# Three edits at once: first loads in pieces, the order of block products and roots at the second norm, and the final norm of a column chunk placed under the next chunk's products

## The chip, the cores and the metric

The kernel runs on one core of a Trainium2 chip. The metric is device time in microseconds (us), from one launch to its end. The core has five engines that run in parallel, each through its own queue of instructions and in that queue's order: TensorE (PE, with its weight loads, PEld), VectorE (DVE), ScalarE (ACT), GpSimd (POOL) and SyncE (SP), which here only issues the transfers. An instruction that waits for a semaphore holds up everything behind it on its engine. TensorE is granted one of two clock levels, 1.2 or 2.4 GHz; the profile gives the granted clock as a share of the full one.

## The reference, cut to what matters

One layer of a decoder step, for a prompt of 1024 tokens and eight samples of eight tokens each, 1088 token columns in all, with a model width of 1024:

```python
h = rms_norm(x, norm_mix_g)                       # first norm
proj = h @ w_in                                   # conv values and gates, q, k, v
...                                               # causal conv head group, dilated attention
x = x + concat([a, o]) @ w_out
h = rms_norm(x, norm_ffn_g)                       # second norm
g = depthwise_conv(concat([past, h @ w_ffn_gate]))
x = x + (silu(g) * (h @ w_ffn_up)) @ w_ffn_down
y = rms_norm(x, norm_final_g)                     # final norm
```

`rms_norm(x, g)` is x times the reciprocal root of the mean square over the 1024 features of a token, times g.

## The kernel before

The activations are held with the features on the 128 partitions and the tokens along the columns, so that x is eight tiles of 128 x 1088. Every product is made of three matmuls with split operands: a "hi" part (`xh`, `wh`, rounded by ACT) and a "lo" part (`xl`, `wl`, the rest, by DVE or POOL), as hi x hi, lo x hi and hi x lo. A block of 1088 columns is cut into column chunks `CHUNKS` of 384, 384 and 320.

**The norms.** The sum of squares over the features is made of squares (ACT, some on POOL) that are added up elementwise over the eight tiles (`sqa`, `sq`; DVE, some on POOL). `root` then sums over the partitions with small matmuls against a column of ones (line 192, out into a bank `ss`, `g2` or `r`), and computes the reciprocal root with some short operations of DVE and one of ACT (lines 194 to 207). `spread` turns the root (`rr`) back into a 128-partition tile `rb` by transposes on PE (line 219) and a copy by ACT (line 221).

**The start.** Lines 263 to 273: SP issues x tile 0, the first block of `w_in` (512 KB in one transfer, by `load_w`), x tile 1, the second block, and the other x tiles, in this order by hand (`tc.issue_after` holds the scheduler to it); three loads of a cache (`cr`, 768 KB each) stand between tiles 4 and 5. Each x tile is split as a whole in `scaled_split`, and each weight block as a whole in `load_w`. `first_gemms` then runs over the eight tiles k, two weight blocks and three chunks: 144 matmuls, 18 for each k. The squares of x tiles 1, 3 and 5 are made on POOL.

**The second norm.** `out_half(h, hook)` makes the output projection of half the columns (544) as eight products m of 12 matmuls (`block_product`, lines 849 to 852, in matmuls of 272 columns), adds each to x (line 982), squares it (line 985) and adds it to the sum of the half (line 989). For the second half, a hook starts work on the norm of the first half: `root` after product m = 1, `spread` after product m = 4 (`norm_first`). What comes next are the first block products of the FFN (`b11h`, `px`, `py`, line 865), which need x scaled by `rb` (line 995). `two_products` fills two such outputs, tile by tile, as the tiles come.

**The end.** The last part of the down projection runs over four column chunks `TAIL` of 256, 256, 320 and 256; for each, `last_product` makes eight products m of 12 matmuls (lines 1262 to 1264), which DVE adds to x (line 1266), ACT squares (line 1268), and DVE and POOL add up in two sums (line 1273) that are joined at the end (line 1274). `last_norm` of a chunk is written in the program behind the next chunk's products; there the scheduler has put it where its operands come. It scales four tiles on DVE (line 1282) and four on POOL and ACT (lines 1284, 1285) and stores each (line 1286). Five banks `g` hold products, two banks `r` the roots.

Of the kernel before, what the change touches and what calls it, by code (L numbers as in the profile page):

```python
# [44 lines left out]
TAIL = ((0, 256), (256, 256), (512, 320), (832, 256))  # L45
# [12 lines left out]
WR = 2  # L58
# [19 lines left out]
def trunk_kernel(tc, xT, w_in, w_out, w_gate, w_up, w_down, par, kc, vc, sa, sf, pmask, smask,  # L78
                 yT, kT, vT, ca, cas, cf):
    nc = tc.nc  # L80
    with (
# [51 lines left out]
        nc.vector.memset(onesc, 1.0 / DC)  # L133

# [49 lines left out]

        def root(sq, div, width):
# [5 lines left out]
            for i, n in enumerate(size):  # L191
                nc.tensor.matmul(ps[:n, i:i + 1], sq[:, i * P:i * P + n], ones, start=True, stop=True)
# [14 lines left out]
            nc.vector.scalar_tensor_tensor(r, t, 1.5, r, op0=ALU.add, op1=ALU.mult)  # L207
            return r

        def spread(r, new, width):  # L210
# [3 lines left out]
            for c0 in range(0, width, 512):  # L214
                pb = bank(*rbank[0])
                w = min(512, width - c0)
                for i in range(c0 // P, -(-(c0 + w) // P)):
                    n = size[i]
                    nc.tensor.transpose(pb[:, i * P - c0:i * P - c0 + n], r[:n, i:i + 1].to_broadcast([n, P]),
                                        ident[:n, :n])  # L220
# [18 lines left out]
        def scaled_split(x, c):  # L239

            hi = zt(main[0], "X", 16, "xh", N, F32R)
            nc.scalar.activation(hi, x, AF.Copy, scale=c)
            lo = zt(main[0], "X", 16, "xl", N, F32R)
            nc.vector.scalar_tensor_tensor(lo, x, c, hi.bitcast(F32), op0=ALU.mult, op1=ALU.subtract)
            return hi, lo
# [17 lines left out]
        x0, w0 = [], []  # L263
        with ExitStack() as order:
            for k in range(KT):
                t = keep("x")
                opened = nc.sync.dma_start(t, xT[k * P:(k + 1) * P, :]).ins
                order.enter_context(tc.issue_after(opened))
                x0.append(t)
                if k in W0:  # L270
                    w0.append(load_w(w_in[2 - 2 * len(w0)], KT, nc.gpsimd if w0 else nc.vector))
        h = [scaled_split(x0[k], col(C_GMIX + k)) for k in range(KT)]
        R = rstd(sum_squares(x0, nc.vector, zbig, (1, 3, 5)), D, zbig)
# [581 lines left out]
        def two_products(outs, ws, x, start, hook=lambda k, last: None):  # L855
# [3 lines left out]
            nk = len(x)  # L859
            for k, (xh, xl) in enumerate(x):  # L860
                for o, (whi, wlo) in zip(outs, ws):
                    for c in range(2):
                        ps = o[:, PO:512] if c == 0 else o[:, 512:PO + HN]
                        t = slice(c * n, c * n + n)
                        nc.tensor.matmul(ps, whi[:, k, :], xh[:, t], start=(start and k == 0), stop=False,
                                         skip_group_check=True)
                        nc.tensor.matmul(ps, whi[:, k, :], xl[:, t], start=False, stop=False, skip_group_check=True)
                        last = nc.tensor.matmul(ps, wlo[:, k, :], xh[:, t], start=False, stop=(k == nk - 1),
                                                skip_group_check=True).ins
                hook(k, last)  # L870
# [385 lines left out]
        def last_product(t0, n):  # L1256
            acc = [None, None]
            for m in range(KT):
                ps = bank(*gbank[0])
                whi, wlo = w[m]  # L1260
                for k, (xh, xl) in enumerate(act):
                    nc.tensor.matmul(ps[:, :n], whi[:, k, :], xh[:, t0:t0 + n], start=(k == 0), stop=False)
                    nc.tensor.matmul(ps[:, :n], whi[:, k, :], xl[:, t0:t0 + n], start=False, stop=False)
                    nc.tensor.matmul(ps[:, :n], wlo[:, k, :], xh[:, t0:t0 + n], start=False, stop=(k == nj - 1))
                x = x2[m][:, t0:t0 + n]
                nc.vector.tensor_add(x, ps[:, :n], x)
                s = wide("sq")[:, :n]
                nc.scalar.activation(s, x, AF.Square)
                i = m % 2
                if acc[i] is None:  # L1270
# [117 lines left out]
```

## Time and profile before

| | before |
|---|---|
| median of 3 runs | 1409.12 us (1405.84 to 1413.22) |
| the profiled execution's own time | 1410.36 us |
| its span, first to last instruction | 1408.6 us |
| busy PE, DVE, ACT, POOL | 96%, 60%, 37%, 32% |
| mean granted TensorE clock | 0.982 |

The span is what the instructions take; 1.76 us of the execution's time lie outside it. PE is busy nearly all of the span, so what matters are the few places where it isn't, and the places at which its clock is at the lower level.

### The profile page before, as it was taken

The page shows a single profiled execution, that of the slowest core. Times are in us where ns is not written, and L with a number is a line of the kernel's source. Part 1 is how long each engine was busy: PE and PEld are TensorE (multiplying, and loading weights), DVE is VectorE, ACT ScalarE, POOL GpSimd, SP SyncE. Part 2 cuts the span into 40 slices and gives each one's busy share as a digit, 9 for nine tenths or more (in the row PEclk, how much of TensorE's full clock was granted, in tenths as well). Part 3 has the DMA queues.
Part 4 walks back from the last instruction along what each step waited for, and adds up shares of the span by engine and source line. Part 5 has one row for each costly group of instructions (what it writes and reads, how often), then busy time and mean ns, then how long its engine had stood idle before and what let it go on. Part 6 is the DMA issues. An engine that isn't in the chain of part 4 may idle for free.

```text
span 1408.6 us, 25028 instructions
## 1 busy us (share of the span) xinstructions
PE 1348.9 (96%) x10059; PEld 1282.0 (91%) x10059; DVE 844.7 (60%) x1636; ACT 521.9 (37%) x1047; POOL 447.0 (32%) x362
## 2 busy tenths in 40 slices
PE   6999999999998999988999999999999999999995
PEld 6988879899977777988999999999999999999995
DVE  7398595556674656677965555665655543322146
ACT  5312212456564564254533333333332332112033
POOL 3221111111001103330754654554654222233124
PEclk9999999999999999998999999999999999999998
DMA  7247676836798878450112222212222672313003
GB/s 275 57 140 248 222 256 206 224 111 168 197 266 229 256 213 257 128 195 24 47 50 89 93 77 77 92 47 77 92 78 77 202 275 60 117 57 123 12 16 113
DMA packets 84884, 195.17 MB, mean 139 GB/s; under 512 B 12576, under 2 KB 46752, under 8 KB 84768
## 3 DMA queue, kind: packets, MB, share of 16 engines
q1 hardware_dynamic: 84768, 193.57, 43.7%
q8 instruction: 79, 1.29, 0.4%
q14 instruction: 37, 0.30, 0.1%
HBM read 145.03 MB, written 48.52 MB: 137 GB/s over the span
## 4 chain that ended last, share of the span: by engine, by line
PE 76%; DVE 10%; issue 5%; DMA 5%; POOL 2%; ACT 1%; SPq 1%; POOLq 0%; DVEq 0%; ACTq 0%
PE g L174 10%; PE g L172 10%; PE g L173 10%; PE py L849 4%; PE py L851 4%; PE py L852 4%; DVE cacc L342 4%; PE o L675 3%; PE s L590 3%; PE pz L852 3%; PE pz L849 3%; PE pz L851 3%; PE px L849 3%; PE px L852 3%; PE px L851 3%
## 5 line engine op out<-in xcount | busy, mean ns | idle before, releaser
L148 POOL TENSOR_TENSOR wl<-wr,wh 128x768 fp32r<-128x768 f32 (+2 forms) x61 | 116.8, 1916 | 461.6 <-PE g L174 373.6
L172 PE MATMUL g<-xh,wh 128*128 128x384 f32 (+1 forms) x472 | 158.1, 335 | 0.0
L173 PE MATMUL g<-xl,wh 128*128 128x384 f32 (+1 forms) x472 | 156.6, 332 | 0.0
L174 PE MATMUL g<-xh,wl 128*128 128x384 f32 (+1 forms) x472 | 156.5, 332 | 0.0
L173 PE MATMUL g<-al,wh 128*128 128x384 f32 (+1 forms) x432 | 143.2, 332 | 1.7 <-DVE al L1203 1.7
L172 PE MATMUL g<-ah,wh 128*128 128x384 f32 (+1 forms) x432 | 141.6, 333 | 2.2 <-ACT ah L1202 0.8
L174 PE MATMUL g<-ah,wl 128*128 128x384 f32 (+1 forms) x432 | 142.7, 332 | 0.7 <-POOL wl L148 0.7
L146 ACT ACTIVATE wh<-wr 128x768 fp32r<-128x768 f32 (+2 forms) x62 | 52.0, 839 | 240.1 <-PE g L174 177.8
L939 POOL TENSOR_TENSOR wb<-wr,wb 128x512 fp32r<-128x512 f32 x84 | 115.2, 1383 | 56.8 <-ACT wb L938 56.8
L1225 DVE TENSOR_TENSOR x<-g,x 128x384 f32<-128x384 f32 (+1 forms) x72 | 38.0, 534 | 137.8 <-PE g L174 137.6
L938 ACT ACTIVATE wb<-wr 128x512 fp32r<-128x512 f32 x84 | 52.4, 628 | 164.2 <-DVE wr L954 105.0
L631 ACT ACTIVATE y<-y,m 128x128 f32<-128x128 f32 (+1 forms) x192 | 88.4, 463 | 32.2 <-DVE m L619 32.1
L1143 DVE SCALAR_TENSOR_TENSOR fc<-gb,prm,fc 128x1104 f32<-128x1104 f32 x44 | 83.5, 1918 | 14.7 <-ACT fc L1141 14.4
L174 PEld LDWEIGHTS g<-xh,wl 128*128 128x128 f32 x472 | 89.3, 189 | 2.6 <-issue 2.5
L172 PEld LDWEIGHTS g<-xh,wh 128*128 128x128 f32 x472 | 89.6, 190 | 1.4 <-issue 1.2
L173 PEld LDWEIGHTS g<-xl,wh 128*128 128x128 f32 x472 | 89.6, 190 | 1.1 <-issue 1.0
L594 DVE CUSTOM_DVE_ANT_0 y<-s,pmk 128x128 f32<-128x128 f32 (+1 forms) x192 | 63.9, 378 | 41.6 <-PE s L590 33.2
L939 POOL TENSOR_TENSOR wa<-wr,wa 128x512 fp32r<-128x512 f32 x42 | 54.9, 1308 | 101.0 <-ACT wa L938 101.0
L172 PEld LDWEIGHTS g<-ah,wh 128*128 128x128 f32 x432 | 81.7, 190 | 3.1 <-ACT ah L1202 1.1
L173 PEld LDWEIGHTS g<-al,wh 128*128 128x128 f32 x432 | 82.1, 190 | 2.4 <-DVE al L1203 2.4
L174 PEld LDWEIGHTS g<-ah,wl 128*128 128x128 f32 x432 | 82.1, 190 | 1.0 <-POOL wl L148 1.0
L342 DVE SCALAR_TENSOR_TENSOR cacc<-gp,prm,cacc 128x1024 f32<-128x1024 f32 x60 | 77.9, 1299 | 0.1
(358 smaller groups left out, 4133.0 us busy)
## 6 DMA issues: line engine op xcount, KB each, us to landing
cr<-in_kc SPq DMA_DIRECT2D x24, 768.0 KB, 8.4
cr<-in_vc SPq DMA_DIRECT2D x24, 768.0 KB, 7.1
kk<-dk SPq DMA_DIRECT2D x48, 256.0 KB, 7.5
u<-u SPq DMA_DIRECT2D x22, 544.0 KB, 3.2
ur<-u SPq DMA_DIRECT2D x22, 544.0 KB, 5.4
wr<-in_w_in SPq DMA_DIRECT2D x22, 512.0 KB, 5.2
wr<-in_w_gate SPq DMA_DIRECT2D x22, 512.0 KB, 3.3
wr<-in_w_up SPq DMA_DIRECT2D x22, 512.0 KB, 5.0
```

The lines of the kernel that those rows point to most:

```text
L148: lo_eng.tensor_sub(lo, raw, hi.bitcast(F32))
L172: nc.tensor.matmul(ps[c], whi[:, k, :], xh[:, t0:t0 + n], start=(k == 0), stop=False)
L173: nc.tensor.matmul(ps[c], whi[:, k, :], xl[:, t0:t0 + n], start=False, stop=False)
L174: nc.tensor.matmul(ps[c], wlo[:, k, :], xh[:, t0:t0 + n], start=False, stop=(k == nk - 1))
L342: eng.scalar_tensor_tensor(acc[:, :S], gp[:, j:j + S], col(w0 + j), acc[:, :S], op0=ALU.mult, op1=ALU.add)
L594: nc.vector.tensor_tensor_reduce(out=y[:, o:o + n], in0=ps[:, o:o + n], in1=mask, op0=ALU.add, op1=ALU.min, scale=1.0, scalar=3e38, accum_ ...
L631: nc.scalar.activation(y, y, AF.Exp, bias=m[:, 4 * g + i:4 * g + i + 1], scale=-1.0, accum_out=den[:, g, 2 * hd + u, i:i + 1])
L849: nc.tensor.matmul(ps, whi[:, k, :], xh[:, t], start=(start and k == 0), stop=False, skip_group_check=True)
L851: nc.tensor.matmul(ps, whi[:, k, :], xl[:, t], start=False, stop=False, skip_group_check=True)
L852: nc.tensor.matmul(ps, wlo[:, k, :], xh[:, t], start=False, stop=(k == nk - 1), skip_group_check=True)
L939: nc.gpsimd.tensor_sub(lo, x, hi.bitcast(F32))
L1143: nc.vector.scalar_tensor_tensor(c[:, :W], gb[i][:, t:t + W], col(C_FW + 3 * f + t), c[:, :W], op0=ALU.mult, op1=ALU.add)
```

## The change

**Start.** x tile 0 is loaded in its three column chunks and the two weight blocks in three pieces each (one, three and four of their eight 128-column parts). Hi and lo of these pieces are made piece by piece (`parts_of_first`, `scaled_split` with `cuts`). An activation on a column of ones, `warm`, stands at ACT's start. All squares are made on ACT.

**Second norm.** `norm_first` calls `root` after product m = 2 and `spread` after m = 5. `two_products` holds its matmuls to the order of the tiles k.

**End.** `TAIL` is 320, 256, 256, 256. The squares of a chunk are added into one sum, all on DVE. The norm of the chunk before is written into the products of a chunk by a hook: `root` after product m = 1, `spread` after m = 3, the scalings after the add of m = 4; six of these are on DVE, those of m = 2 and 5 on POOL and ACT. The last chunk's eight scalings are all on DVE. `tc.issue_after` holds PE's and DVE's work to this order.

```diff
-TAIL = ((0, 256), (256, 256), (512, 320), (832, 256))
+TAIL = ((0, 320), (320, 256), (576, 256), (832, 256))
...
+        nc.scalar.activation(sp.tile([P, 1], F32, name="warm"), ones, AF.Copy)
...
-        def scaled_split(x, c):
+        def scaled_split(x, c, cuts=((0, N),)):
...
+            for t0, n in cuts:
+                t = slice(t0, t0 + n)
+                nc.scalar.activation(hi[:, t], x[:, t], AF.Copy, scale=c)
+                nc.vector.scalar_tensor_tensor(lo[:, t], x[:, t], c, hi.bitcast(F32)[:, t], op0=ALU.mult,
+                                               op1=ALU.subtract)
...
+            load_x(0, CHUNKS[:1])
+            load_first(0, 0, 1)
+            load_x(0, CHUNKS[1:])
+            load_first(1, 0, 1)
+            load_first(0, 1, 4)
+            load_first(1, 1, 4)
+            load_x(1)
+            load_x(2)
+            load_x(3)
+            load_first(0, 4, KT)
+            load_first(1, 4, KT)
+            for k in range(4, KT):
+                load_x(k)
...
+        def parts_of_first(i, k, e):
+            c = slice(k * P, e * P)
+            hi, lo = w0[i]
+            nc.scalar.activation(hi[:, c], wr[i][:, c], AF.Copy)
+            (nc.gpsimd if i else nc.vector).tensor_sub(lo[:, c], wr[i][:, c], hi.bitcast(F32)[:, c])
...
-        R = rstd(sum_squares(x0, nc.vector, zbig, (1, 3, 5)), D, zbig)
+        R = rstd(sum_squares(x0, nc.vector, zbig), D, zbig)
...
             for k, (xh, xl) in enumerate(x):
...
+                with tc.issue_after(last) if last else nullcontext():
...
-            if m == 1:
+            if m == 2:
                 rs.append(root(sq0, D, HN))
-            elif m == 4:
+            elif m == 5:
                 rs[0] = spread(rs[0], new_root, HN)
...
-                    (nc.vector if i else nc.gpsimd).tensor_add(acc[i], s, acc[i])
-            nc.vector.tensor_add(acc[0], acc[1], acc[0])
...
+                    added, late = late if m > 1 else None, nc.vector.tensor_add(acc, s, acc).ins
+                hook(m, last.ins, reduced)
...
+                if m == 1:
+                    with tc.issue_after(last):
+                        r.append(root(acc, D, chunk[1]))
+                elif m == 3:
+                    with tc.issue_after(last):
+                        r[0] = spread(r[0], wide, chunk[1])[:, :chunk[1]]
+                elif m == 4:
+                    with tc.issue_after(reduced):
+                        scaled(r[0], *chunk, others=(2, 5))
...
+        scaled(rstd(acc, D, wide, n)[:, :n], *TAIL[-1])
```

How the instructions stand on the engines, before and after, at three places (line numbers are those of the kernel that the row is of; the numbers in a name are the tile and its use).

SP's queue at the start of the program, of before: `prm` are the small parameters, `x_1` is x tile 0, `x_5` tile 1, `wr_2` and `wr_6` the two weight blocks.

```order
L129 DMA prm_74<-in_par 128x180
L267 DMA x_1_100<-in_xT 128x1088
L143 DMA wr_2_102<-in_w_in 128x1024
L267 DMA x_5_108<-in_xT 128x1088
L143 DMA wr_6_110<-in_w_in 128x1024
L267 DMA x_9_116<-in_xT 128x1088
L267 DMA x_10_118<-in_xT 128x1088
L267 DMA x_11_120<-in_xT 128x1088
L156 DMA cr_112_914<-in_kc 128x1536
```

The same place on SP after the change; here `wr_9` and `wr_10` are the weight blocks, `x_2` is x tile 1.

```order
L278 DMA x_1_102<-in_xT 128x384
L278 DMA wr_9_110<-in_w_in 128x128
L278 DMA x_1_102<-in_xT 128x384
L278 DMA x_1_102<-in_xT 128x320
L278 DMA wr_10_111<-in_w_in 128x128
L278 DMA wr_9_110<-in_w_in 128x384
L278 DMA wr_10_111<-in_w_in 128x384
L278 DMA x_2_103<-in_xT 128x1088
L278 DMA x_3_104<-in_xT 128x1088
L278 DMA x_4_105<-in_xT 128x1088
L278 DMA wr_9_110<-in_w_in 128x512
L278 DMA wr_10_111<-in_w_in 128x512
```

The first matmul's operands now stand in the first two transfers behind `prm`, of 384 and 128 columns, where before they were two of 1088 and 1024; three x tiles stand ahead of the rest of the weights, and the three cache loads come two x tiles later (behind tile 5).

PE in `out_half`, second half, around the small matmuls of the first half's root (`g2` <- `ones`, `sq`), of before: the product ahead of them is m = 1.

```order
L849 MATMUL g_1271_6860<-mh_1227_6634,wh_1230_6640 128x272
L851 MATMUL g_1271_6860<-ml_1228_6635,wh_1230_6640 128x272
L852 MATMUL g_1271_6860<-mh_1227_6634,wl_1231_6641 128x272
L192 MATMUL g2_1273_6878<-ones_76,sq_1254_6715 128x1 x4
L192 MATMUL g2_1273_6878<-ones_76,sq_1254_6715 32x1
L849 MATMUL g_1277_6895<-mh_1224_6628,wh_1232_6644 128x272
L851 MATMUL g_1277_6895<-ml_1225_6629,wh_1232_6644 128x272
L852 MATMUL g_1277_6895<-mh_1224_6628,wl_1233_6645 128x272
```

The same place on PE after the change: the product ahead is m = 2.

```order
L893 MATMUL g_1273_6898<-mh_1227_6654,wh_1232_6664 128x272
L895 MATMUL g_1273_6898<-ml_1228_6655,wh_1232_6664 128x272
L896 MATMUL g_1273_6898<-mh_1227_6654,wl_1233_6665 128x272
L195 MATMUL g2_1275_6916<-ones_76,sq_1254_6735 128x1 x4
L195 MATMUL g2_1275_6916<-ones_76,sq_1254_6735 32x1
L893 MATMUL g_1279_6933<-mh_1224_6648,wh_1232_6664 128x272
L895 MATMUL g_1279_6933<-ml_1225_6649,wh_1232_6664 128x272
L896 MATMUL g_1279_6933<-mh_1224_6648,wl_1233_6665 128x272
```

The root's matmuls stand 12 matmuls, one whole product, later in PE's queue than before.

PE at the very end of the program, of before: the last two matmuls of the last chunk's products, and then the roots and spreads (`r`) of the last two chunks.

```order
L1263 MATMUL g_2043_14522<-al_1920_13497,wh_1931_13524 128x256
L1264 MATMUL g_2043_14522<-ah_1919_13496,wl_1932_13525 128x256
L192 MATMUL r_2045_14540<-ones_76,sq_2008_14246 128x1 x2
L192 MATMUL r_2045_14540<-ones_76,sq_2008_14246 64x1
L219 MATMUL r_2050_14556<-ident_69,rr_2047_14548 128x128 x2
L219 MATMUL r_2050_14556<-ident_69,rr_2047_14548 128x64
L192 MATMUL r_2051_14581<-ones_76,sq_2030_14419 128x1 x2
L219 MATMUL r_2056_14595<-ident_69,rr_2053_14587 128x128 x2
```

After the change the root of the last chunk but one (`r_2033` <- `sq_2008`) stands on PE behind product m = 1 of the last chunk (`g_2031`):

```order
L1313 MATMUL g_2031_14440<-al_1920_13517,wh_1922_13523 128x256
L1314 MATMUL g_2031_14440<-ah_1919_13516,wl_1923_13524 128x256
L195 MATMUL r_2033_14457<-ones_76,sq_2008_14267 128x1 x2
L1312 MATMUL g_2037_14470<-ah_1910_13498,wh_1925_13530 128x256
L1313 MATMUL g_2037_14470<-al_1911_13499,wh_1925_13530 128x256
```

On DVE, in the last chunk after the change, the scalings of the chunk before (line 1341, six tiles) stand behind the add of product m = 4 (`x2_1806` <- `g_2043`), and ahead of the sum and the adds of m = 5 and 6:

```order
L1324 TENSOR_TENSOR x2_1799_12466<-g_2039_14487,x2_1799_12466 128x256
L1330 TENSOR_TENSOR sq_2030_14438<-sq_2040_14501,sq_2030_14438 128x256
L1324 TENSOR_TENSOR x2_1806_12534<-g_2043_14509,x2_1806_12534 128x256
L1341 SCALAR_TENSOR_TENSOR x2_1760_12226<-x2_1760_12226,prm_74,rb_2041_14504 128x256
L1341 SCALAR_TENSOR_TENSOR x2_1767_12294<-x2_1767_12294,prm_74,rb_2041_14504 128x256
L1341 SCALAR_TENSOR_TENSOR x2_1799_12466<-x2_1799_12466,prm_74,rb_2041_14504 128x256
L1341 SCALAR_TENSOR_TENSOR x2_1806_12534<-x2_1806_12534,prm_74,rb_2041_14504 128x256
L1341 SCALAR_TENSOR_TENSOR x2_1820_12670<-x2_1820_12670,prm_74,rb_2041_14504 128x256
L1341 SCALAR_TENSOR_TENSOR x2_1827_12738<-x2_1827_12738,prm_74,rb_2041_14504 128x256
L1330 TENSOR_TENSOR sq_2030_14438<-sq_2044_14523,sq_2030_14438 128x256
L1324 TENSOR_TENSOR x2_1813_12602<-g_2045_14544,x2_1813_12602 128x256
L1324 TENSOR_TENSOR x2_1820_12670<-g_2047_14561,x2_1820_12670 128x256
```

Of the two norms that stood wholly behind the last product, one is now inside the last chunk's products; only the last chunk's own root and spread are left behind them. Everywhere else the order of the five engines is the same as before.

## Rows read from the trace of the kernel before

**Rows 1.** The page's chain that ended last: shares of the span by engine.

```profile
PE 76%; DVE 10%; issue 5%; DMA 5%; POOL 2%; ACT 1%; SPq 1%; POOLq 0%; DVEq 0%; ACTq 0%
```

**Rows 2.** Waits of PE: line, releaser: us in total, times, longest us.

```profile
PE r L219 <- DVE rr L207: 8.1, 2, 5.5
```

**Rows 3.** Timeline from 0 us: start, duration, instruction, idle before and its releaser.

```profile
1.18 0.42 SPq L267 DMA_DIRECT2D x<-in_xT  x1
...
6.08 1.28 ACT L242 ACT_TABLE_LOAD   x1 [6.08 <-DMA x<-in_xT]
...
9.48 1.04 ACT L146 ACTIVATE wh<-wr 128x1024 fp32r<-128x1024 f32 x1
...
10.57 0.69 PE L283 MATMUL g<-xh,wh 128*128 128x384 f32 x1 [10.57 <-ACT wh L146]
...
12.34 0.52 PE L283 MATMUL g<-xh,wh 128*128 128x384 f32 x1
...
12.66 0.52 PE L284 MATMUL g<-xl,wh 128*128 128x384 f32 x1
```

**Rows 4.** Transfers issued from 0 to 45 us: KB each, median us to landing.

```profile
x<-in_xT SPq DMA_DIRECT2D x8, 544.0 KB, 7.3
...
prm<-in_par SPq DMA_DIRECT2D x1, 90.0 KB, 2.0
```

**Rows 5.** Stretch: PE, PEld, DVE, ACT, POOL busy (x), clock, DMA share, GB/s.

```profile
15.00:20.00 5.00, 5.00 (x30) 5.00 (x29) 5.00 (x3) 1.37 (x2) 3.20 (x2) 1.00 1.01 414
```

**Rows 6.** Groups by shape, 0 to 40 us: busy us, mean ns, idle before.

```profile
L244 DVE SCALAR_TENSOR_TENSOR xl<-x,prm,xh 128x1088 fp32r<-128x1088 f32 x8 | 16.5, 2056 | 7.5 <-ACT xh L242 7.5
...
L290 ACT ACTIVATE gp<-g 128x384 f32<-128x384 f32 x2 | 0.9, 478 | 0.0
```

**Rows 7.** Timeline from 33 to 40 us, the end of the first products.

```profile
33.33 1.34 DVE L244 SCALAR_TENSOR_TENSOR xl<-x,prm,xh 128x1088 fp32r<-128x1088 f32 x1
...
34.60 1.28 DVE L236 TENSOR_TENSOR sqa<-sq,sqa 128x1088 f32<-128x1088 f32 x1
...
37.33 0.34 PE L285 MATMUL g<-xh,wl 128*128 128x384 f32 x1
...
37.51 0.31 PE L284 MATMUL g<-xl,wh 128*128 128x320 f32 x1
...
37.80 2.04 PE L192 MATMUL ss<-ones,sqa 128*128 128x1 f32 x18
```

**Rows 8.** Timeline around the second norm's first root.

```profile
618.47 0.29 PE L852 MATMUL g<-mh,wl 128*128 128x272 f32 x1
...
622.41 1.20 PE L192 MATMUL g<-ones,sq 128*128 128x1 f32 x10 [3.65 <-DVE sq L989]
```

**Rows 9.** The same view of stretches, behind that root.

```profile
624.00:626.00 2.00, 2.00 (x11) 2.00 (x11) 1.16 (x7) 0.21 (x2) 1.11 (x1) 0.50 0.38 143
...
628.00:630.00 2.00, 2.00 (x19) 1.96 (x17) 1.55 (x3) 0.80 (x2) 0.00 (x0) 1.00 0.42 163
```

**Rows 10.** Timeline at the first FFN block product.

```profile
638.79 0.60 PE L865 MATMUL px<-b11h,wa 128*128 128x272 f32 x1 [3.71 <-DVE x L995]
```

**Rows 11.** Timeline of the last 20 us.

```profile
1389.69 0.28 PE L1264 MATMUL g<-ah,wl 128*128 128x256 f32 x1
...
1389.81 0.71 PE L192 MATMUL r<-ones,sq 128*128 128x1 f32 x6
...
1398.68 0.15 DVE L201 RECIPROCAL rr<-rv 128x2 f32<-128x2 f32 x1
...
1400.98 3.64 DVE L1282 SCALAR_TENSOR_TENSOR x<-x,prm,rb 128x256 f32<-128x256 f32 x4 [1.32 <-ACT rb L221]
```

**Rows 12.** Groups by shape, 1339 to 1409 us.

```profile
L1282 DVE SCALAR_TENSOR_TENSOR x<-x,prm,rb 128x256 f32<-128x256 f32 x12 | 10.7, 951 | 2.1 <-ACT rb L221 2.1
L1284 POOL TENSOR_TENSOR x<-x,rb 128x256 f32<-128x256 f32 x12 | 10.1, 874 | 13.6 <-ACT rb L221 13.6
...
L1266 DVE TENSOR_TENSOR x<-g,x 128x256 f32<-128x256 f32 x24 | 10.0, 422 | 13.0 <-PE g L1264 12.4
```

More of the change, by code (lines that the diff above doesn't have):

```diff
@@ L9 @@
-from contextlib import ExitStack, contextmanager
+from contextlib import ExitStack, contextmanager, nullcontext
 import numpy as np
@@ L191, in root @@
             for i, n in enumerate(size):
[L192 removed]
+                summed[0] = nc.tensor.matmul(ps[:n, i:i + 1], sq[:, i * P:i * P + n], ones, start=True, stop=True).ins
             v = sp.tile([P, 9], F32, tag="rv", name=nm("rv"), bufs=2)[:, :nt]
@@ L268, in trunk_kernel, with load_x @@
                 order.enter_context(tc.issue_after(opened))
[L269 to L272, printed above, removed]
-        R = rstd(sum_squares(x0, nc.vector, zbig, (1, 3, 5)), D, zbig)
+            def load_x(k, cuts=((0, N),)):
+                for t0, n in cuts:
+                    load(x0[k][:, t0:t0 + n], xT[k * P:(k + 1) * P, t0:t0 + n])
@@ L859, in two_products @@
             nk = len(x)
+            last = None
             for k, (xh, xl) in enumerate(x):
[L861 to L869, printed above, removed]
+                with tc.issue_after(last) if last else nullcontext():
+                    for o, (whi, wlo) in zip(outs, ws):
+                        for c in range(2):
+                            ps = o[:, PO:512] if c == 0 else o[:, 512:PO + HN]
+                            t = slice(c * n, c * n + n)
+                            nc.tensor.matmul(ps, whi[:, k, :], xh[:, t], start=(start and k == 0), stop=False,
+                                             skip_group_check=True)
+                            nc.tensor.matmul(ps, whi[:, k, :], xl[:, t], start=False, stop=False,
+                                             skip_group_check=True)
+                            end = nc.tensor.matmul(ps, wlo[:, k, :], xh[:, t], start=False, stop=(k == nk - 1),
+                                                   skip_group_check=True).ins
+                last = end
                 hook(k, last)
@@ L1260, in last_product @@
                 whi, wlo = w[m]
[L1261 to L1264, printed above, removed]
-                x = x2[m][:, t0:t0 + n]
-                nc.vector.tensor_add(x, ps[:, :n], x)
+                with tc.issue_after(summed[0]) if m in (2, 4) and i else nullcontext():
+                    for k, (xh, xl) in enumerate(act):
+                        nc.tensor.matmul(ps[:, :n], whi[:, k, :], xh[:, t0:t0 + n], start=(k == 0), stop=False)
+                        nc.tensor.matmul(ps[:, :n], whi[:, k, :], xl[:, t0:t0 + n], start=False, stop=False)
+                        last = nc.tensor.matmul(ps[:, :n], wlo[:, k, :], xh[:, t0:t0 + n], start=False,
+                                                stop=(k == nj - 1))
@@ L1267, in last_product @@
+                x = x2[m][:, t0:t0 + n]
+                with ExitStack() as order:
+                    if m == 3 and i:
+                        order.enter_context(tc.issue_after(rooted[0]))
+                    if m > 4 and scalings:
+                        order.enter_context(tc.issue_after(scalings[-1]))
+                    if m > 2:
+                        order.enter_context(tc.issue_after(added))
+                    reduced = nc.vector.tensor_add(x, ps[:, :n], x).ins
                 s = wide("sq")[:, :n]
```

67 lines of the change are left out of this document (41 added, 26 removed).

## The prediction

> **What bounds the kernel now.** I read the page's chain first: PE is three quarters of it, DVE, issue and DMA are the rest [rows 1]. A kernel in which PE is busy 96% of the span gains only where PE stands still or runs at its lower clock level, so I went to PE's waits and to the timeline at each of them, and asked which the change touches. There are three.
>
> At the start PE waits 10.57 us for its first operand [rows 3]. The steps to it are to be seen in the timeline: x tile 0 is issued at 1.18 and lands at 6.08, a table load of 1.28 then stands on ACT ahead of everything, behind it the hi part of x, a square, and the hi part of a whole weight block (1.04 us, from 9.48) [rows 3].
>
> At the second norm, PE has run out of products at 618.6 and waits 3.65 us for the first half's sum of squares, at 622.41 [rows 8]. The clock falls behind it: in a stretch with a granted clock of 0.50 (the 1.2 GHz level) 11 matmuls ran, in one at 1.00 there were 19 [rows 9]. The last product before the wait was of m = 1; those of m = 2 and later had their operands and a free pair of banks all along.
>
> At the end the last matmul of the products starts at 1389.69 [rows 11] and the span ends at 1408.6: 18.8 us in which PE does next to nothing. The waits of `spread` for the root (8.1 us, two of them, the longer 5.5) are here [rows 2]: two norms, one behind the other, each with four scalings on DVE, those of the second from 1400.98 for 3.64 us [rows 11].
>
> **The start.** The first matmul now needs 192 KB of x and 64 KB of weights. How soon these land no row shows. The 90 KB of parameters landed 2.0 us after their issue, x tile 0 with 544 KB 4.9 us after it (6.08 - 1.18) [rows 3, 4]. Between these by bytes, the 192 KB take 2.7 us; with the parameters ahead of them and the weight piece behind I take 3.6, so 4.8 us of the span. ACT's table load is now made by `warm` while nothing else is there to do. The hi part of 128 x 384 is one ACT instruction of about 0.48 [rows 6], that of 128 x 128 weights lies below it: 0.3. PE starts at 5.7 instead of 10.57, **4.9 us earlier**. Bounds: 3.8 + 0.6 = 4.4 if bytes alone decide; 6.08 + 0.8 = 6.9 if the pieces land no sooner than the whole tile does now.
>
> Does the rest keep up? From 10.57 to 37.80 the 144 matmuls take 27.2 us [rows 3, 7]. At the end they start 0.18 us apart (384 columns) and 0.145 (320) [rows 7], so one k takes 12 x 0.18 + 6 x 0.145 = 3.0; early on they are 0.32 apart [rows 3], and that costs 27.2 - 24 = 3 us. After the change the first k runs slow just as well (18 matmuls at about 0.32), so I keep the 27.2. DVE needs 1.34 + 1.28 for each k when nothing disturbs it [rows 7], less than PE's 3.0; now its split takes 2.06 in the mean [rows 6], and the three squares that leave POOL can only lower that. ACT gets these three: 18 instructions of about 1.04 [rows 3] are 19 us of 27. The transfers up to x tile 7, with the cache loads ahead of it, are 7.7 MB, at 414 GB/s [rows 5] 18.6 us; with issue and landing it is there by 22 to 25, and PE wants it at 32.9 - 3.0, less 2.6 for the split: 27. That cover is thin for tile 6 but it holds. Behind the first products the order is unchanged, and R, with which DVE's next work begins, comes from the same sums, earlier by as much.
>
> **The second norm.** One more product ahead of the root fills the wait with 12 matmuls: 12 x 2.00 / 19 = 1.3 us [rows 9]. The wait shrinks from 3.65 to some 2.3. PE still stands, so the clock may still fall; I count half a microsecond for less of it: **-1.8 us**. Bounds: nothing, if the sum's chain on DVE is delayed by the add of that product; and 3.65 + 1.0 (eight matmuls lost in the slow stretch, 8 x 0.105, and a little more) if the wait closes. The wait of 3.71 us ahead of the FFN's first block product [rows 10] comes from the second half's last sums and scalings, which don't move. `spread` comes one product later, which still leaves its result ahead of its readers, the second half's last two products being behind it.
>
> **The end.** PE's products now carry three roots and spreads instead of two; each is an instruction group of about 0.7 at most [rows 11], and I add 0.5 for a wait of the root in one chunk: +1.1. What lies behind the last product, step by step:
>
> 1. DVE's arrears. The scalings of the chunk before are queued behind the add of m = 4. PE then has three products left, 36 matmuls 0.12 apart [rows 11]: 4.3 us. DVE has four adds of 0.42 [rows 12], four sums, which I price like the adds, and six scalings. One scaling took 0.95 with POOL's multiplies beside it [rows 12]; free of them it should take no more than an add of that width, 0.42, which has also two inputs. Only two of eight tiles are POOL's now; I take 0.55. 8 x 0.42 + 6 x 0.55 = 6.7, which is 2.4 more than PE's 4.3.
> 2. Root and spread: from the reciprocal to the first scaling 2.3 (1398.68 to 1400.98) [rows 11], and 0.6 ahead of it for the sums over partitions: 2.9.
> 3. Eight scalings on DVE alone, 8 x 0.42 = 3.4.
> 4. From the last scaling to the span's end, now 1408.6 - 1404.62 = 4.0 [rows 11]; unchanged.
>
> Together 12.7 instead of 18.8: -6.1, and with the 1.1 within the products **-5.0 us**. Bounds by the scalings' price: at 0.42 it is -5.8, and without the 0.5 of wait -6.3; at 0.95 it is -2.6.
>
> The Trainium skill ("SBUF — State Buffer", "Who interferes with whom") says more: a VectorE instruction with two SBUF inputs and a GpSimd instruction that reads SBUF exclude each other, the later one standing for the whole of the earlier. The 0.95 against 0.42 agrees in kind. By that rule two multiplies of 0.87 [rows 12] could each cost their full length, 6 x 0.42 + 1.7 = 4.3 in place of my 3.3, and the sum would be a microsecond less.
>
> **Sum.** -4.9 - 1.8 - 5.0 = -11.7 us on a span of 1408.6: 1396.9. The profiled execution took 1410.36, 1.24 more than the median, so the median goes from 1409.12 to **1397.4**.
>
> **Rivals.**
>
> *The pieces don't come sooner, or PE starves between them.* Six more transfers are issued ahead of x tile 7, each 0.42 us of SP [rows 3], so x tile 1 could come 2.5 us late; and a PE that waits between its first few matmuls would stay at the slow spacing for a second k, 18 x (0.32 - 0.17) = 2.7. Then the start gives 4.9 - 5.2, nothing: 1402. For it: the row of 7.3 us for a tile [rows 4] shows transfers queueing for one another. Against it: PE's first k alone takes over 5 us, in which 2 MB arrive. The Trainium skill ("DMA: Bandwidth & Descriptors", "Rules for kernel authors") has the rule for this rival: coalesce, since under 64 KB a transfer is mostly overhead. The weight pieces lie at that mark; the nearest row, 90 KB in 2.0 us, is against a great loss. 0.12.
>
> *The clock gives more.* PE's wait at the root falls so short that the clock holds, and the scalings run at 0.42: -4.9 - 4.6 - 6.3 = -15.8, 1393. 0.08.
>
> *DVE becomes the bound under the last products.* Per chunk it has 8 adds and 7 sums at 0.42, the root's six short operations at 0.15 [rows 11] and six scalings: 7.2 + 6 s, where PE has 96 matmuls at 0.12 and the root, 12. It decides at s = 0.8. At s = 0.95 DVE needs 0.9 more than PE in each of three chunks, and the banks run full: -4.9 - 1.8 - 2.6 + 2.7 = -6.6, 1402.5. Against it: only two multiplies on POOL. 0.08.
>
> *The enforced order makes PE wait in each chunk: slower.* The root's matmuls stand on PE behind m = 1, and now must not be passed. If the last sum of the chunk before isn't there, all products stand. If that goes as at the second norm, 3.65 and 1.0 of clock, three chunks cost 14, and the kernel is slower by 2: 1411. It breaks even at a wait of 2.9 us a chunk, and is clearly slower from 5. For it: DVE's arrears of some 2.4 at a chunk's end; against it: products m = 0 and 1 take 2.9 to 3.5 us, which cover them. 0.04.
>
> *It does nothing:* waits that go here come back in the next stretch that waits for a transfer, 1407. PE was busy between these places, so little of this. 0.04.
>
> **How the numbers follow.** My forecast holds 0.64. Its own range, from the sums of half the bounds, is 1393.5 to 1401. To reach the rivals on both sides until two in ten are left out I give **1391 to 1402.5**. A difference under 0.5%, 7 us, can't be told from none: that is at 1402.1. Below it lie the forecast, the clock case and two thirds of the first rival; in the band a third of that, DVE as the bound, the last rival and half of the enforced order: faster 0.81, same 0.16, slower 0.03.
>
> **What would show it.** PE's first matmul at 5 to 7 us and the sums over partitions at 32 to 34; the root's wait at the second norm near 2.3 and the wait for the first block product still near 3.7; in the tail no wait over 1 us in PE, 12 to 13 us from the last product to the end, the scalings at 0.42 to 0.6. Wrong would be: a first k with gaps for `x` or `wr`; a split on DVE still at 2 us; PE waiting for DVE in each of the last chunks.

## The result, and the profile after

The changed kernel takes 1393.66 us (median of 4 runs, 1387.1 to 1398.29) where the kernel before took 1410.22 on the same chip: a ratio of 0.9887, 95% interval 0.9856 to 0.9919. Six more runs, beside the last experiments, gave 0.988 (0.9852 to 0.9908). That is some 16 us; 11.7 were forecast, and 1391 to 1402.5 as the range. The profiled execution has a span of 1393.4 us, 15.2 less than before.

The page of the kernel after, busy times and the chain that ended last:

```profile
PE 1346.9 (97%) x10059; PEld 1280.3 (92%) x10059; DVE 835.9 (60%) x1662; ACT 521.7 (37%) x1047; POOL 423.4 (30%) x339
...
PE 79%; DVE 10%; DMA 7%; issue 1%; ACT 1%; SPq 1%; POOL 0%; DVEq 0%; ACTq 0%; POOLq 0%
```

PE's share of the chain went from 76 to 79% [rows 1], and DMA's from 5 to 7%: a first hint that the transfers at the start hold more up than they did.

**The start**, timeline of the kernel after:

```profile
3.85 0.61 ACT L248 ACTIVATE xh<-x,prm 128x384 fp32r<-128x384 f32 x1 [1.63 <-DMA x<-in_xT]
...
4.72 0.69 PE L327 MATMUL g<-xh,wh 128*128 128x384 f32 x1 [4.72 <-ACT wh L305]
...
10.93 1.20 ACT L248 ACTIVATE xh<-x,prm 128x1088 fp32r<-128x1088 f32 x1 [0.95 <-DMA x<-in_xT]
...
12.19 0.61 PE L327 MATMUL g<-xh,wh 128*128 128x384 f32 x2 [1.30 <-ACT xh L248]
...
34.94 0.31 PE L329 MATMUL g<-xh,wl 128*128 128x320 f32 x1
...
35.09 1.06 PE L195 MATMUL ss<-ones,sqa 128*128 128x1 f32 x9
```

PE begins 5.85 us earlier than in [rows 3], but the sums over partitions stand at 35.09, only 2.7 earlier than in [rows 7]. The rows show one of the places where the rest went: x tile 1 lands just ahead of 10.93, and PE waits 1.30 us for its hi part.

**The second norm**, timeline and stretches of the kernel after (the stretch's columns are those of [rows 5]):

```profile
617.36 1.35 PE L195 MATMUL g<-ones,sq 128*128 128x1 f32 x10 [1.67 <-DVE sq L1037]
...
632.16 0.59 PE L911 MATMUL px<-b11h,wa 128*128 128x272 f32 x1 [3.66 <-DVE x L1043]
```

```profile
618.00:620.00 2.00, 2.00 (x12) 1.97 (x12) 2.00 (x4) 1.88 (x2) 2.00 (x2) 0.53 0.98 359
620.00:622.00 2.00, 2.00 (x12) 2.00 (x12) 1.02 (x3) 0.21 (x1) 0.07 (x1) 0.62 0.52 161
622.00:624.00 2.00, 2.00 (x18) 2.00 (x17) 1.63 (x7) 0.66 (x1) 0.00 (x0) 1.00 0.73 281
```

The root's wait is 1.67 us instead of 3.65 [rows 8], the wait ahead of the FFN stays (3.66, was 3.71 [rows 10]). The clock still falls to the 1.2 GHz level behind the root.

**The end**, timeline, and the scalings by shape, of the kernel after:

```profile
1381.52 0.28 PE L1314 MATMUL g<-ah,wl 128*128 128x256 f32 x1
...
1383.95 0.58 PE L195 MATMUL r<-ones,sq 128*128 128x1 f32 x4 [2.15 <-DVE sq L1330]
1384.56 0.16 DVE L199 TENSOR_SCALAR rv<-r 128x2 f32<-128x2 f32 x1 [0.76 <-PE r L195]
...
1385.89 0.47 PE L222 MATMUL r<-ident,rr 128*128 128x128 f32 x2 [1.37 <-DVE rr L210]
...
1386.88 3.25 DVE L1341 SCALAR_TENSOR_TENSOR x<-x,prm,rb 128x256 f32<-128x256 f32 x8 [1.13 <-ACT rb L224]
```

```profile
L1341 DVE SCALAR_TENSOR_TENSOR x<-x,prm,rb 128x256 f32<-128x256 f32 x20 | 9.3, 531 | 1.1 <-ACT rb L224 1.1
```

From one spacing (0.12 us) behind the start of the last matmul, 1381.64, to the end of the span it is 11.8 us; by the same count it was 18.8. Two waits of PE are left in the tail: 2.15 for the last sum and 1.37 for the root.

### The profile page after: what moved, and what is told of

The parts are those of the page before. It is cut to its first block, busy times and chain, and to the rows that moved or that the text cites. A ratio compares the mean times of both kernels' runs of the same rounds, so it can differ in the third digit from the quotient of the medians.

```text
span 1393.4 us, 25044 instructions
## 1 busy us (share of the span) xinstructions
PE 1346.9 (97%) x10059; PEld 1280.3 (92%) x10059; DVE 835.9 (60%) x1662; ACT 521.7 (37%) x1047; POOL 423.4 (30%) x339
## 4 chain that ended last, share of the span: by engine, by line
PE 79%; DVE 10%; DMA 7%; issue 1%; ACT 1%; SPq 1%; POOL 0%; DVEq 0%; ACTq 0%; POOLq 0%
PE g L175 9%; PE g L174 9%; PE g L173 9%; PE py L895 4%; PE py L893 4%; PE py L896 4%; DVE cacc L386 4%; PE o L719 3%; PE pz L895 3%; PE pz L896 3%; PE pz L893 3%; PE px L893 3%; PE px L895 3%; PE px L896 3%; PE s L634 3%; PE t L702 2%
```

## The experiments

A profiled execution differs from the next by several us in stretches that no edit touches, so each kernel was read in two ways: by its timing, and by the length of three stretches of its trace, each between the starts of two instructions that all kernels have. "First products" is the start of their last matmul, counted from 0; in the four kernels with a star the scheduler has put the 18 small matmuls of the sums ahead of the last products, and their 2.0 us are taken off. "Norm" goes from the first add of `out_half` to DVE's first split for `b22l`; "tail" from the last 384-wide add of the down projection to the end of the span.

| kernel | first products | norm | tail | ratio to before (95%) |
|---|---|---|---|---|
| before | 37.65 | 54.74 | 71.18 | |
| before, second trace | 36.54 | 55.27 | 71.21 | |
| start alone | 35.15 | 54.93 | 71.00 | 0.9948 (0.9929 to 0.9968) |
| norm alone | 36.53 | 50.98 | 71.41 | 0.9974 (0.9953 to 0.9995) |
| tail alone | 36.52 | 55.25 | 65.74 | 0.9975 (0.9957 to 0.9993) |
| root's move alone | 36.97 | 52.63 | 71.34 | 0.9984 (0.9965 to 1.0004) |
| change without start | 37.04 | 50.97 | 65.69 | 0.9929 (0.9900 to 0.9958) |
| change | 34.94 | 50.33 | 65.59 | 0.9887 (0.9856 to 0.9919) |
| change again | 36.69 | 50.72 | 65.77 | 0.9880 (0.9852 to 0.9908) |
| change, cache loads last | 35.7* | 53.28 | 65.71 | 0.9922 (0.9897 to 0.9948) |
| change, whole weights | 34.0* | 53.23 | 66.01 | 0.9937 (0.9916 to 0.9959) |
| change, start whole | 34.2* | 51.36 | 65.68 | 0.9910 (0.9875 to 0.9946) |
| change, root later | 34.79 | 48.46 | 65.70 | 0.9902 (0.9876 to 0.9929) |
| combined | 35.7* | 48.47 | 68.03 | 0.9915 (0.9889 to 0.9941) |

**Before, unchanged.** No edit; one more execution, for a second trace.

> The kernel before, unchanged, for a second trace of it. Theory: stretches that the change does not touch differ by a few us from one execution to the next (the down projection from 1135 to 1334 us took 199.3 us in the first trace of before and 196.5 after the change, with the same instructions), so this trace too moves by up to 4 us against the first one outside the three places. Rival: the trace repeats within 1 us in each stretch, and the gains outside the three places belong to the change.

It ended 3.2 us sooner than the first trace. Nearly all of that arose between the attention's products and the output projection: from DVE's multiply of one chunk of q, k or v by `rb` (at 300.95 us in the first trace) to the projection's first 384-wide add it took 249.99 us, in the first trace 253.34. So the theory held, and the rival (each stretch repeats within 1 us) fell. Over all fourteen traces this stretch has values from 246.4 to 257.2, with and without each part of the change. What a single pair of traces shows there is chance, and a gain must be read in its own stretch or timed. Most of this chance is the clock. Here is the stretch in the shortest trace (norm alone) and in the longest (change, whole weights); the number 1.00 or 0.97 is the mean granted clock:

```profile
300.29:546.69 246.40, 242.19 (x2053) 203.25 (x2052) 154.43 (x586) 145.63 (x428) 28.59 (x24) 1.00 0.76 220
```

```profile
298.44:555.63 257.19, 247.86 (x2053) 207.44 (x2052) 155.58 (x585) 145.52 (x428) 28.24 (x24) 0.97 0.75 211
```

TensorE was at the lower level for none of the first and for 13.7 us of the second (0 to 17.1 us over the fourteen traces). If half of that time counts as lost, the fourteen values lie between 246.4 and 250.8.

**The three parts, each alone.** The edits are the three groups of the diff above: `warm`, pieces and squares; `two_products` and `norm_first`; `TAIL`, `last_product` and the hook.

> The first part alone: loads in pieces, early table load, squares on ACT. Theory from the trace after the change: PE starts 5.9 us earlier (4.7 instead of 10.57), but the sums over partitions come only 2.7 earlier and the products behind them 1.0 to 1.5, because the pieces slow the transfers (275 GB/s from 5 to 10 us, before 421) and later x tiles and weights come late; so the kernel gains 1 to 2 us, ratio 0.999. Rival, as predicted: 4.9 us, ratio 0.9965.

> The second part alone: root after product 2, spread after product 5, and the tile order of the first block products. Theory from the trace after the change: the wait at the root falls from 3.65 to 1.7 us, the clock falls for as long as before, and the block products behind it come 2.5 to 3 us earlier; ratio 0.998. Rival, as predicted: 1.8 us. A third: nothing, if the next stretches take it back.

> The third part alone: the final norm of a chunk under the next chunk's products. Theory: from the last product to the end 11.8 us instead of 18.8, the products 1 to 1.5 us longer, so 5 to 6 us gained, ratio 0.996. Rival: no less than 9 us, so that the three parts alone make up the 15 us between the two profiled executions.

The three ratios multiply to 0.9897, near the 0.9887 and 0.988 of the whole: the parts add up. By its timing the norm alone gives 3.7 us (0.7 to 6.6) and the tail alone 3.5 (1.0 to 6.1), which agrees with the stretches below; the rival of 9 us for the tail fell. The tail's stretch is 5.5 us shorter with that part in it, whatever else is in the kernel, as long as the tail's chunks are those of the change. The norm's is 55.0 without that part (four traces) and 50.3 to 53.3 with it (eight traces with the root behind product 2). For the start my theory was wrong in its size: the timing gives 7.3 us (4.5 to 10), so that the rival's 4.9 lies inside the interval and the theory's 1 to 2 doesn't. The first products, though, show no more than 1.4 to 2.5.

**The change without its start.**

> The change without its first part (second norm and tail only). Theory (the start is worth 1.5 us to the block products, as the traces say): ratio to before 0.994 to 0.995, and no more than 2 us above the whole change of this call. Rival (the start is worth 7 us, as its own timing said): 6 to 8 us above the whole change.

0.9929 against 0.9880 for the whole change on the same chip: about 7 us by the ratios, 4.9 by the medians, with an uncertainty of some 5 in the difference. So the second timing too makes the start worth more than its own stretch shows.

**The change again.**

> The changed kernel again, on the chip of this call, for more executions of it. Theory: the first four executions lay low by chance; 0.991, as the local gains of the three parts give it (1.5 + 2.5 + 5.5 us of 1409, and 2 us of clock). Rival: 0.9887 again.

The rival held: 0.988 again. The sum of local gains (1.5 + 3.4 + 5.5, below) falls some 6 us short of it.

**Cache loads behind the x tiles.**

```diff
-            cached.append(nc.sync.dma_start(t, src).ins)
+            with tc.issue_after(opened):
+                cached.append(nc.sync.dma_start(t, src).ins)
```

> The changed kernel with the three cache loads behind all x tiles on SP (before and in the change they stand between tiles 5 and 6). In the changed kernel PE starts at 4.7 us, but its 144 first products take 30.4 us instead of 27.2, and ACT waits for x tile 6 until 24.8. Theory A (x tiles come late because of what stands ahead of them in the queue): tiles 6 and 7 come 4 to 5 us sooner, PE's pause near 21 to 24 us goes, the sums over partitions come at 33 to 34 instead of 35.1, and the kernel gains about 1 us on the changed one, ratio to before 0.988. Rival B (the small pieces have slowed the transfers, and only the wait for tile 1 matters): the sums stay at 35.

Tile 6 was no longer late, but the last of the first products came at 37.65, or 35.7 without the sums that stand ahead of it here: no sooner than in the change. The timeline of this kernel has the reason, once more PE waiting for tile 1 and then for a split; and the weights for the next products now come later, behind the cache:

```profile
11.86 0.61 PE L328 MATMUL g<-xh,wh 128*128 128x384 f32 x2 [2.12 <-ACT xh L249]
...
20.62 0.45 PE L329 MATMUL g<-xl,wh 128*128 128x384 f32 x1 [1.18 <-DVE xl L250]
```

```profile
31.48 1.06 ACT L147 ACTIVATE wh<-wr 128x1024 fp32r<-128x1024 f32 x1 [5.05 <-DMA wr<-in_w_in]
```

The sums themselves stood at 32.70, which looks like theory A's gain and is not: a milestone is only one where its place in the order is the same. Theory A fell. The late tile 6 wasn't what held the products up.

**Whole weight blocks, and the whole start.** The first edit loads the weight blocks in one transfer each, with x tile 0 in pieces still; the second loads x tile 0 whole as well and makes hi and lo of each as a whole, so that `warm` and the squares on ACT are all that is left of the first part.

```diff
             load_x(0, CHUNKS[:1])
-            load_first(0, 0, 1)
+            load_first(0, 0, KT)
             load_x(0, CHUNKS[1:])
-            load_first(1, 0, 1)
...
             load_x(1)
+            load_first(1, 0, KT)
```

```diff
-            load_x(0, CHUNKS[:1])
-            load_first(0, 0, 1)
...
+            load_x(0)
+            load_first(0, 0, KT)
+            load_x(1)
+            load_first(1, 0, KT)
```

> The changed kernel with the two first weight blocks loaded whole (512 KB each) again, x tile 0 still in three pieces, x tile 1 ahead of the second block. Theory B (pieces with rows of 512 and 1536 bytes slow the transfers): from 5 to 10 us 400 GB/s or more instead of 275, x tile 1 lands before 10 us, PE starts about 1.5 us later (6 to 6.5) and yet the sums come at 34.5 or sooner. Theory A (it is the order, not the size): 275 to 300 GB/s as in the change, and sums at 36 or later because PE starts later.

> The change with x tile 0 and both first weight blocks whole, in the order of before; of the first part the early table load and the squares on ACT are left. Theory (the pieces bring PE 4 us earlier to its first matmul but only 1.5 of it to the end of the first products, and the squares and the table load have a part in that): PE starts at 8.5 to 9.5, the sums come at 36.5 to 37.5, between before and the change. Rival (the pieces only slow the transfers): the sums come at 35 or sooner, as early as with the pieces.

The stretch from 5 to 10 us in the kernel before, the change, the change with whole weights, and with the start whole, in this order (one view, four kernels):

```profile
5.00:10.00 5.00, 0.00 (x0) 0.00 (x0) 1.39 (x1) 3.91 (x4) 1.35 (x1) 1.00 1.03 421
```

```profile
5.00:10.00 5.00, 5.00 (x16) 4.26 (x17) 1.96 (x5) 3.20 (x6) 0.46 (x1) 1.00 0.95 275
```

```profile
5.00:10.00 5.00, 3.66 (x10) 2.58 (x10) 2.56 (x6) 4.51 (x8) 0.00 (x0) 1.00 1.02 355
```

```profile
5.00:10.00 5.00, 1.35 (x4) 1.35 (x5) 2.72 (x3) 4.55 (x5) 0.00 (x0) 1.00 1.02 413
```

The last number is GB/s, the one ahead of it the share of time in which the transfer engines were busy. They are busy nearly all the time in each row, and move 421, 275, 355 and 413: the smaller the first transfers (64 to 192 KB in the change), the less is moved in the same busy time. Theory B has the direction right; its 400 GB/s came only with x tile 0 whole as well. The rows of PE that go with it, of the kernel with the start whole:

```profile
8.65 0.69 PE L316 MATMUL g<-xh,wh 128*128 128x384 f32 x1 [8.65 <-ACT wh L298]
...
36.22 0.31 PE L318 MATMUL g<-xh,wl 128*128 128x320 f32 x1
```

PE starts 4 us later than in the change, and its products end at 34.2 when the sums in their midst are taken off; with whole weights it starts at 5.66 and they end at 34.0. With all pieces and the order of the change they end between 34.79 and 36.69 (four traces). Taking off the sums alone overlooks that in these two kernels some of the root's transposes come ahead of the next products too, after a wait of some 1.5 us. A place behind these, the 36th matmul of the next products, gives the same reading: it starts at 45.1 and 45.3 in these two, at 45.8 in the mean of the four traces with all pieces (44.0 to 47.5) and at 46.8 in that of the six without the first part (45.7 to 47.7). So the pieces bought PE an early start and gave all of it back: what the first part gains in its own stretch is already there with the early table load and the squares on ACT alone (which no run takes apart), and the rival of the last expectation held. Yet neither kernel beats the change by its timing: 0.9910 overlaps with it, and 0.9937 lies above.

**The root's move alone.** The kernel before, with this edit only:

```diff
-            if m == 1:
+            if m == 2:
...
-            elif m == 4:
+            elif m == 5:
```

> Before with the root after product 2 and the spread after product 5 alone, without the tile order of the block products. Theory: the root's move is the whole of the second part, wait 2.1 us as with both, ratio about 0.9975. Rival: the tile order carries a part of it, then this stays at 0.9985 or above, and the block products from 631 to 660 us run in another order with more waits.

The root's wait is 2.2 us as with the tile order (2.1). The norm's stretch is 52.63, which lies among the kernels that have both; the tile order shows no gain of its own that these runs can tell.

**The root one product later.**

```diff
-            if m == 2:
+            if m == 3:
```

> The changed kernel with the root after product 3 (spread still after product 5). Theory: one more product, 1.5 us, fills the wait at the root, which falls from 1.7 to 0.2 or so, and with no pause the clock does not fall there: 2 us or more gained on the changed kernel, 0.987. Rival: the root then comes too late for the spread, PE waits 1 us or more at the spread in its place, and the time stays at 0.9887.

Here is the clearest row of the study. Stretches of this kernel around the root, at 622.27, and under them those of before, second trace, where the root is at 618.66:

```profile
620.00:622.00 2.00, 1.99 (x16) 1.77 (x15) 2.00 (x4) 1.69 (x4) 0.43 (x1) 1.00 0.72 186
622.00:624.00 2.00, 1.73 (x15) 1.74 (x16) 2.00 (x4) 1.22 (x3) 2.00 (x2) 1.00 0.68 180
624.00:626.00 2.00, 2.00 (x19) 2.00 (x18) 2.00 (x5) 1.42 (x2) 0.99 (x1) 1.00 0.94 341
```

```profile
618.00:620.00 2.00, 1.34 (x8) 1.36 (x8) 1.53 (x2) 1.98 (x3) 2.00 (x2) 0.78 0.93 259
620.00:622.00 2.00, 2.00 (x11) 1.98 (x11) 1.32 (x8) 0.46 (x2) 1.35 (x1) 0.50 0.48 183
622.00:624.00 2.00, 2.00 (x11) 2.00 (x11) 0.68 (x1) 0.00 (x0) 0.00 (x0) 0.50 0.76 260
624.00:626.00 2.00, 2.00 (x10) 2.00 (x10) 0.05 (x1) 0.66 (x1) 0.00 (x0) 0.51 0.36 141
```

With a wait of 0.28 at this root the granted clock stays at 1.00; with 3.65 the clock is at the lower level for 6.8 us (a mean of 0.78 in a stretch of 2 us is 0.88 us at 0.50, and so on: 0.88 + 2 + 2 + 1.96). PE then waits 1.08 at the spread, so both my theory and its rival hold in part, and that wait too leaves the clock up. It isn't one lucky execution: in all twelve traces with a wait of 1.67 to 3.71 at this root the clock falls around its end, for 3.4 or 6.8 us, and in the two with the root behind product 3 (0.28 here, 0.76 in the last kernel) it doesn't. The norm's stretch is 48.46, 6.5 shorter than before and 1.9 to 4.8 shorter than with the root behind product 2. In time this can't be told from the change (0.9902 against 0.9887 and 0.9880).

**Combined.** The loads of "whole weights" above, and

```diff
-TAIL = ((0, 320), (320, 256), (576, 256), (832, 256))
+TAIL = ((0, 320), (320, 320), (640, 256), (896, 192))
...
-            if m == 2:
+            if m == 3:
...
-            elif m == 5:
+            elif m == 6:
```

> The change with whole weight blocks at the start (x tile 0 in pieces, x tile 1 ahead of the second block), root after product 3 and spread after product 6, and the tail's chunks 320, 320, 256 and 192. Expected if the readings hold: sums over partitions at 34 us, no wait over 0.5 us at the root or the spread and the wait ahead of the first block product below 4; behind the last product 10.5 us instead of 11.8, as DVE has eight scalings of 192 columns less; in all 2 to 4 us below the whole change of this call. Rival: a late spread moves its wait to the first block product, which then waits 5 us or more, and PE waits for sums in the last, shorter chunk; no gain.

The norm is as good as with the root behind product 3 and an earlier spread (48.47). The waits at root and spread were 0.76 and 0.72 where 0.5 at most was expected, and the one ahead of the first block product 4.02 instead of 3.66, so the rival's 5 didn't come. But the tail took 68.03, 2.3 longer than the change's. Two matmuls of the last chunk:

```profile
1378.52 0.27 PE L1306 MATMUL g<-ah,wh 128*128 128x192 f32 x1
1378.63 0.27 PE L1307 MATMUL g<-al,wh 128*128 128x192 f32 x1
```

192 columns start 0.11 us apart where 256 take 0.12 [rows 11]: the chunk that lost a quarter of its columns kept nine tenths of its time, and the columns it gave away cost their full price in the chunk of 320. The products took 53.9 us instead of 51.3, and what lies behind them came out 0.2 shorter, where 1.3 was expected. 0.9915: no gain, as the rival had it.

## Why the prediction was right, and where it was not

The direction, the place of each gain and the range held, and the time came out 3.7 us below the value. The steps one by one:

**The tail: right, in each of its steps.** Forecast -5.0, measured -5.5 (tail alone 65.74 against 71.2). DVE's arrears of 2.4 are PE's wait of 2.15 for the last sum; root and spread of 2.9 are 1383.95 to 1386.88, 2.9; eight scalings of 3.4 took 3.25; the six beside GpSimd's multiplies were priced at 0.55 each, 3.3, and took 3.00 in the last chunk. (The 531 ns in the row above is a mean over these six, six of an earlier chunk and the last eight, which nothing disturbs.) What was off is small: the end behind the last scaling took 3.3 instead of 4.0, and the products grew by 1.5 (51.3 against 49.8, first to last start) instead of 1.1. The rows of the six scalings and of the two multiplies:

```profile
1377.86 3.00 DVE L1341 SCALAR_TENSOR_TENSOR x<-x,prm,rb 128x256 f32<-128x256 f32 x6
```

```profile
1377.16 1.44 POOL L1338 TENSOR_TENSOR x<-x,rb 128x256 f32<-128x256 f32 x2 [10.71 <-ACT rb L224]
```

Only the second multiply ran beside the scalings: the first of these took 1.02, the other five 0.47 each, so one multiply of 0.74 cost some 0.55. The rule of the Trainium skill ("SBUF — State Buffer", "Who interferes with whom"), that a GpSimd instruction can make a scaling wait for its whole length, is near that for the one pair that met. The 4.3 that the prediction worked out by it counted both multiplies, and the first was nearly over before the scalings began.

The rivals "DVE becomes the bound" and "the enforced order makes PE wait" didn't come: PE's waits in the tail are the two behind the last product.

**The second norm: the mechanism right, a term too small.** Forecast -1.8; the mean of the eight kernels with the root behind product 2 is 51.69 against 55.05, so -3.4. The root's wait was right: 1.67 to 3.02 us in the eight, 2.3 in the mean as forecast, against 3.5 in the mean of the four without, which is the 1.3 of the sum. The step that was mis-sized is "I count half a microsecond for less of it", the clock. All four kernels without this part have 13.7 us at the lower level within the stretch, though they divide it differently (at the root 3.4 us in the first trace of before and 6.8 in the second, after the same wait of 3.65). Of the eight with it five have some 10.3 and three 13.7; in the change it was 3.4 at the root (the stretches at 0.53 and 0.62: 1.88 + 1.52) and 6.8 behind the later wait. 3.4 us less is worth half of its length, 1.7, in five of eight kernels, so 1.1 in the mean. The last 1.0 of the 3.4 no row accounts for. The Trainium skill ("TensorE: Matmul & The Clock Gate", "What's actually happening") says of a kernel's first matmuls that the number of slow ones differs from run to run; these traces show it behind a wait in the middle of a kernel too. Of the 3 us between the 50.3 and the 53.3 that stand in one column, the clock is 1.7.

**The start: the step "does the rest keep up" failed.** PE starts at 4.7 (forecast 5.7, within its bounds). The 27.2 us for the 144 matmuls, which I kept, became 30.4 (4.72 to 35.09), and 32.2 in the trace of the change again. PE waits for x tile 1 (1.3 us, and 3.1 in that other trace), which I had landing in time since I took 414 GB/s for all transfers, pieces too; the row for the pieces is 275. It waits 1.2 for a split on DVE near 20.9, too. And in two of the four traces with the pieces and the change's order the clock fell in the wait for tile 1 or soon behind it; these are the stretches of the change again, where that wait ends at 13.21:

```profile
12.00:14.00 2.00, 0.79 (x2) 0.79 (x3) 0.81 (x1) 2.00 (x2) 0.15 (x1) 0.53 1.03 384
14.00:16.00 2.00, 2.00 (x8) 2.00 (x8) 2.00 (x3) 2.00 (x3) 0.00 (x0) 0.50 1.04 425
16.00:18.00 2.00, 2.00 (x9) 2.00 (x8) 2.00 (x2) 2.00 (x3) 0.00 (x0) 0.50 1.04 432
18.00:20.00 2.00, 2.00 (x11) 2.00 (x10) 1.90 (x3) 2.00 (x4) 0.53 (x1) 0.77 1.00 414
```

That is 6.8 us at the lower level; with the start alone it was 3.4, behind a wait of 1.46. None of the three kernels with whole weight blocks shows a fall there. So the last of the first products comes at 35.4 in the mean of the four traces with the pieces and the change's order, and at 36.9 in the mean of six without the first part: 1.5 instead of 4.9, and by the kernel with the start whole these 1.5 don't come from the pieces. The rival that the pieces starve PE was right in its mechanism, its second term (slow matmuls behind the wait) included, and took some 70% of the forecast gain. The rule of the Trainium skill cited beside it ("DMA: Bandwidth & Descriptors", "Rules for kernel authors"), to coalesce, points the same way, though it puts the mark at 64 KB: here transfers of 64 to 192 KB brought the rate down by a third.

**What stays open.** By timing the start is worth 7.3 (alone) and about 7 (change with and without it), by its own stretch 1.5. Some 6 us of the whole gain are thus in no stretch that I can name: neither in the first products, nor in the norm or the tail, and the stretches between show no difference beyond the scatter of single traces, which is larger than this (246.4 to 257.2 in the attention alone; with half of the time at the lower level taken off, its mean is 248.0 in the four traces with the pieces and the change's order, 248.6 in the six without the first part). The kernels with larger first loads end their first products sooner and yet stand at 0.991 to 0.994. The clock isn't the answer for most of it: the mean granted clock is 0.982 in the six runs of the start alone and in the 23 of before that were timed beside them, 0.985 and 0.983 in the change with and without its start, and 0.001 is at most 1.4 us. Whether the order of the first transfers changes what the attention's transfers meet later, or both timings lay on one side, these runs don't tell. So the total came out near the forecast partly by luck: a gain that wasn't forecast stands where a forecast one failed.

## What to carry to other kernels

Move a root or another small dependent chain far enough behind products that PE doesn't stand still: behind the wait the slow clock can cost about as much again (here 1.7 or 3.4 us behind waits of 1.7 to 3.7), and at this root that part vanished only where the wait was below 0.8. An earlier first matmul is worth nothing by itself; cost the operands of the second and third tile at the rate of the pieces, not of the large transfers. In a tail, count the work of the engine that sums and scales against what PE still has to do, instruction by instruction at its undisturbed duration: it gave each step here to within 0.7 us.

## What the runs showed of the hardware

- A pause of PE of 1.7 to 3.7 us at the second norm's root came with 3.4 or 6.8 us at a granted clock of 0.50, from about its end, in twelve traces of twelve; pauses of 0.28 and 0.76 there, and of 0.72 and 1.08 at the spread, with none. The length of a pause alone doesn't decide it: at the start of the program pauses of 1.46 and 3.12 came with a fall, those of 1.30, 1.69 and 2.12 with none.
- The transfer engines were busy for 0.95 to 1.03 of the stretch from 5 to 10 us in four kernels, and moved 421, 413, 355 or 275 GB/s by the size of the first loads: a full share of busy time says nothing of the rate.
- Matmuls of 192 columns start 0.11 us apart, those of 256 columns 0.12.
